# Another instruction order in the opening of a two-layer attention backbone, with five operands read from PSUM by ScalarE

## The chip, the core and the metric

The kernel runs on one core of a Trainium2 chip. The metric is the device time of one execution in microseconds (us); lower is better. Engines: TensorE (PE; its weight loads are PEld), VectorE (DVE), ScalarE (ACT), GpSimd (POOL) and SyncE (SP), which issues most of the DMA transfers. Each engine takes its instructions strictly in the order of its own queue and waits at the first whose semaphore has not come.

## The reference

Two layers over 1024 latent tokens (`x`) and 256 context tokens (`ctx`), model width 1024. Layer 0 is windowed attention with sink logits, layer 1 is latent attention. Cut to what the change touches:

```python
for i in range(DEPTH):
    shift_x, scale_x, gate_x = adaln(c, ada_w[i], ada_b[i])          # silu(c) @ ada_w + ada_b
    shift_c, scale_c, gate_c = adaln(c_ctx, ada_w[i], ada_b[i])
    hx = rms_norm(x, norm_g[i]) * (1.0 + scale_x[:, None]) + shift_x[:, None]
    hc = rms_norm(ctx, norm_g[i]) * (1.0 + scale_c) + shift_c
    yx, yc = window_gqa(hx, hc, a_w_in[j], ...)    # begins with q, k, v, g = split(h @ w_in)
    x = x + gate_x[:, None] * yx
    ...
```

All arithmetic is in float32. The products are made of a high part (rounded to the matmul's short format, `fp32r`) and a low part (the rest): high by high, high by low and low by high.

## The kernel before

The **opening** makes the normalized, conditioned and transposed input `h` of layer 0 for all tokens, and beside it the value projection `v`, the first 256 columns of the input projection. Tokens are worked in five blocks `p` of 256 (block 0 is the context), the 1024 features in four quarters `b`, so there are 20 **groups** `(p, b)`. The list `groups` (L932) gives their order: (0,0) (1,0) (2,0) (0,1) (1,1) (2,1) (3,0) (3,1) (4,0) (4,1), then the quarters 2 and 3 of all blocks.

For one block: `x_load` (L854) brings two tiles of 128 tokens, `square` (L860, ScalarE) and `norm` (L865, a small VectorE operation and a power on GpSimd) make the inverse root mean square, `scale` (L870, one half on VectorE or ScalarE each) applies it.

For one group there are four steps:

- `turn` (L877): four TensorE transposes into one PSUM bank, 5 or 7.
- `h_part` (L884): VectorE reads the bank twice, once for each 128 features (L890), times the scale plus the shift of the conditioning, into a buffer `h` in SBUF. Then one copy of all 512 columns (L892, ScalarE or GpSimd) makes the high part.
- `h_low` (L895): `h` minus the high part is the low part (L897, VectorE or GpSimd).
- `v_part` (L899): twelve matmuls, eight with the high part (L906) and four with the low part (L911).

Scale and shift of a quarter `q` come from a **conditioning step**: `ada_load` (L829) brings four pieces of `ada_w`, `ada_mm` (L835) multiplies each piece (four matmuls, L839), `ada_copy` (L843) moves the sums to SBUF on ScalarE, `ada_cols` (L846) spreads them as columns with two matmuls (L849) and three small VectorE operations (L328, L331). A group of quarter `q` can't pass `h_part` before `ada_cols(q)`. `w0_cut` (L927) splits two rows of the weights of `v` into high and low parts.

The opening stands between L947 and L1056 in a manual schedule: each engine gets its instructions in the order in which the code is written there, the two loops over the groups included; `make(i)` (L936) stands for the turn, the parts and the lows of the group `i`. A recording planner that orders instructions by costs (`Plan`, L68) is only switched on later (L1062). Tile's semaphores are set by the framework: it makes an engine wait for an earlier user of the same PSUM bank too.

After the opening come the other projections of layer 0 (matmuls L285 to L287), the attention, and layer 1.

## Time and profile before

| | |
|---|---|
| median of 3 runs | 1489.08 us (1487.2 to 1856.97) |
| profiled execution | 1487.75 us |
| its span, first to last instruction | 1485.6 us |
| TensorE, VectorE, ScalarE, GpSimd busy | 98%, 71%, 50%, 54% |
| products of groups in the opening (L906, L911) | 18.9 to 70.4 us |

How to read the rows: a timeline row has the start, the length, the engine, the line, the operation, what it writes and reads, and the count; in brackets stands the idle time of the engine before it and what ended that. A row of a group of instructions has its count, then its busy time and the mean of one in ns. A matmul's row lasts until its modelled end, so rows of TensorE that follow each other overlap a little, and the distance of two starts tells more than the lengths. A float32 matmul is recorded twice: a conditioning step's four matmuls of each of its four pieces are 32 records.

### The profile page before, as it was taken

How to read it: one execution, taken by the hardware profiler on the slowest of the kernel's cores; microseconds unless marked ns; L12 is line 12 of the kernel's file. 1: busy time of each engine (PE TensorE's matmuls, PEld its weight loads, DVE VectorE, ACT ScalarE, POOL GpSimd, SP SyncE). 2: the span in 40 equal slices, each digit the busy share in tenths (PEclk: the TensorE clock that was granted, in tenths of full speed). 3: DMA queues.
4: the chain of work that ended last, by engine and by line, in shares of the span. 5: the costliest groups of instructions: out<-in, count | busy, mean ns of one | idle time of the engine just before them, and what ended most of it. 6: DMA issues, size and time to landing. Idle time of an engine off the chain costs nothing.

```text
span 1485.6 us, 25066 instructions
## 1 busy us (share of the span) xinstructions
PE 1462.1 (98%) x9036; PEld 1186.8 (80%) x9036; DVE 1060.5 (71%) x2025; ACT 737.5 (50%) x1401; POOL 808.6 (54%) x735
## 2 busy tenths in 40 slices
PE   6999999999999999999999999999999999999998
PEld 4888888888888888889888888767777767866687
DVE  3787789648778888877988777666576466556764
ACT  4421222359888878877554432443454344444321
POOL 2563366356454444456300240798788788789371
PEclk9999999999999999999999999999999999999999
DMA  9545644573343333337344566011112212120442
GB/s 334 173 166 175 212 146 174 186 245 110 122 140 121 104 100 100 97 98 257 101 118 120 169 236 201 23 44 49 50 61 69 61 47 62 54 68 28 154 148 86
DMA packets 146964, 186.01 MB, mean 125 GB/s; under 512 B 12812, under 2 KB 100492, under 8 KB 146840
## 3 DMA queue, kind: packets, MB, share of 16 engines
q1 hardware_dynamic: 141864, 177.75, 37.9%
q10 hardware_dynamic: 4976, 6.66, 1.3%
q8 instruction: 71, 1.16, 0.3%
q14 instruction: 53, 0.43, 0.1%
HBM read 134.02 MB, written 46.15 MB: 121 GB/s over the span
## 4 chain that ended last, share of the span: by engine, by line
PE 90%; DVE 4%; DMA 2%; issue 1%; ACT 1%; POOL 0%; POOLq 0%; DVEq 0%; ACTq 0%
PE PB L285 14%; PE PB L286 14%; PE PB L287 14%; PE PB L1791 13%; PE PB L1814 9%; PE PB L737 5%; PE PB L1757 5%; PE PB L727 5%; PE PB L697 3%; PE PB L698 3%; DMA arena_f<-ada_w 1%; PE PB L1825 1%; PE PB L906 1%; DVE arena_r L281 1%; PE PB L756 1%
## 5 line engine op out<-in xcount | busy, mean ns | idle before, releaser
L285 PE MATMUL PB<-arena_r 128*128 128x512 f32 (+2 forms) x1200 | 439.4, 366 | 1.1 <-DVE arena_f L1239 1.1
L286 PE MATMUL PB<-arena_r 128*128 128x512 f32 (+2 forms) x1200 | 433.7, 361 | 0.0
L287 PE MATMUL PB<-arena_r 128*128 128x512 f32 (+2 forms) x1200 | 433.3, 361 | 0.0
L1807 POOL TENSOR_TENSOR arena_f<-arena_f 128x1024 f32<-128x1024 f32 x120 | 285.9, 2383 | 8.2
L285 PEld LDWEIGHTS PB<-arena_r 128*128 128x128 f32 x1200 | 226.3, 189 | 45.7 <-issue 9.0
L287 PEld LDWEIGHTS PB<-arena_r 128*128 128x128 f32 x1200 | 226.3, 189 | 33.5
L286 PEld LDWEIGHTS PB<-arena_r 128*128 128x128 f32 x1200 | 226.4, 189 | 32.1 <-POOL arena_r L281 0.6
L1791 PE MATMUL PB<-arena_r 64*128 64x512 f32 (+1 forms) x1600 | 229.3, 395 | 0.0
L1801 ACT ACTIVATE arena_f<-PB 128x1024 f32<-128x1024 f32 x160 | 164.5, 1028 | 111.7 <-PE PB L1791 84.9
L1763 DVE TENSOR_REDUCE krF<-PB 128x1 f32<-128x512 f32 (+1 forms) x264 | 166.9, 677 | 65.6 <-PE PB L1757 65.6
L1791 PEld LDWEIGHTS PB<-arena_r 64*128 64x128 f32 (+1 forms) x1600 | 178.2, 185 | 15.7 <-issue 5.2
L704 DVE CUSTOM_DVE_ANT_0 arena_f<-PB,arena_f,small 128x256 f32<-128x256 f32 (+1 forms) x288 | 148.1, 524 | 51.4 <-PE PB L698 32.8
L280 ACT CAST arena_r<-PB 128x512 fp32r<-128x512 f32 (+2 forms) x207 | 115.3, 563 | 113.2 <-PE PB L287 73.3
L281 DVE TENSOR_TENSOR arena_r<-PB,arena_r 128x512 fp32r<-128x512 f32 (+2 forms) x207 | 134.2, 660 | 35.1 <-ACT arena_r L280 34.4
L1814 PE MATMUL PB<-arena_f 128*64 128x512 f32 x640 | 146.0, 595 | 0.0
L281 POOL TENSOR_TENSOR arena_r<-arena_f,arena_r 128x512 fp32r<-128x512 f32 (+1 forms) x64 | 87.7, 1386 | 105.2 <-ACT arena_r L280 91.0
L280 ACT CAST arena_r<-arena_f 128x512 fp32r<-128x512 f32 (+1 forms) x142 | 82.3, 610 | 90.2 <-PE PB L287 27.8
L710 ACT ACTIVATE arena_f<-arena_f,small 128x640 f32<-128x640 f32 (+2 forms) x160 | 119.1, 745 | 15.8 <-DVE small L704 13.7
L507 DVE SCALAR_TENSOR_TENSOR arena_f<-arena_f,small 128x512 f32<-128x512 f32 x98 | 114.9, 1217 | 10.5 <-DMA arena_f<-ada_w 10.3
L737 PE MATMUL PB<-arena_r 128*128 128x512 f32 x336 | 118.7, 429 | 0.0
L1757 PE MATMUL PB<-arena_r 64*128 64x512 f32 (+1 forms) x768 | 113.9, 355 | 0.1
L727 PE MATMUL PB<-ident,arena_f 128*128 128x128 f32 x672 | 108.7, 272 | 0.1
(216 smaller groups left out, 2083.0 us busy)
## 6 DMA issues: line engine op xcount, KB each, us to landing
arena_f<-ada_w SPq DMA_DIRECT2D x96, 256.0 KB, 4.1
arena_r<-q_d SPq DMA_DIRECT2D x160, 128.0 KB, 2.8
arena_f<-a_w_in SPq DMA_DIRECT2D x40, 256.0 KB, 4.1
arena_f<-b_w_in SPq DMA_DIRECT2D x36, 256.0 KB, 3.3
arena_f<-x SPq DMA_DIRECT2D x16, 512.0 KB, 6.4
q_d<-arena_f SPq DMA_DIRECT2D x16, 512.0 KB, 3.0
arena_r<-qn_d SPq DMA_DIRECT2D x16, 512.0 KB, 5.1
g_d<-arena_f ACTq DMA_DIRECT2D x20, 256.0 KB, 4.1
```

Source lines behind the costliest of these rows:

```text
L280: nc.scalar.copy(hi, src)
L281: (lo_eng or nc.vector).tensor_sub(lo, src, hi.bitcast(F32))
L285: nc.tensor.matmul(o, ah, bh, start=first, stop=False)
L286: nc.tensor.matmul(o, al, bh, start=False, stop=False)
L287: nc.tensor.matmul(o, ah, bl, start=False, stop=last)
L727: nc.tensor.transpose(pt[:, h, :], self.Ps[h][:, ci * 128 : ci * 128 + 128], ident)
L737: nc.tensor.matmul(self.pv, V[:, self.chunks[ci], self.g, :], PT[:, s], start=ci == 0 and s == 0, stop=ci == self.m - 1 and s == 1,)
L1757: nc.tensor.matmul(bank[:, o : o + n], self.q[r, s, bs], k[r, 0, n0 : n0 + n], start=s == 0, stop=s == 2)
L1763: nc.vector.reduce_max(self.mxp[:, e, b : b + 1, i], bank[:, 0:n], AX.X)
L1791: nc.tensor.matmul(PB[:, b + e, :], k[r, s, cs], q[r, sq], start=i == 0, stop=i == 4)
L1807: eng.tensor_add(acc, acc, E)
L1814: nc.tensor.matmul(PB[r, 7, :], Vq[:, c, h, :], E[:, e], start=c == 0, stop=c == NT - 1)
```

## The change

- `h_part` gets two more forms. With `hi=None` ScalarE makes the high part itself, out of the PSUM bank (an `Identity` activation with scale and bias, one for each 128 features), beside VectorE's reading of the same bank into `h`. With `parts=2` the copy is made in two halves. Five groups take the first form: (1,0), (2,0), (0,1), (2,1) and (3,0). Group (0,0) takes the second, on GpSimd.
- `turn` and `v_part` run their inner loops in the other order: transposes token tile by token tile, high products feature block by feature block.
- `square` and `norm` can be done for one half of a block; blocks 1 and 2 use that.
- The order in the opening is rewritten up to group 8. Turn (1,1) stands ahead of the columns of conditioning step 1; the third conditioning step (`q = 2`) stands in one block behind the product of group (3,1), and turns (4,0) and (4,1) follow it, which stood behind the products of (3,0) and (3,1); the lows of (1,0), (1,1), (2,1) and (3,1) are made by VectorE, `w0_cut(1)` wholly by GpSimd.

SyncE's queue is the same in both. The lines of the helpers move: in the changed kernel L892 is ScalarE's reading of the bank, L894 and L897 are the copies, L902 the low part, L911 the high products and L916 the low products.

```diff
-    def norm(p):
+    def norm(p, j=0, n=2):
         _, sq, st = xn[p]
-        nc.vector.tensor_scalar(st[:, 0:2], sq[:, 0:2], 1.0 / D, EPS, ALU.mult, ALU.add)
-        nc.gpsimd.tensor_tensor(st[:, 2:4], st[:, 0:2], mhalf.to_broadcast([128, 2]), ALU.pow)
+        nc.vector.tensor_scalar(st[:, j : j + n], sq[:, j : j + n], 1.0 / D, EPS, ALU.mult, ALU.add)
+        nc.gpsimd.tensor_tensor(st[:, 2 + j : 2 + j + n], st[:, j : j + n], mhalf.to_broadcast([128, n]), ALU.pow)
...
-    def h_part(p, b, hi=nc.scalar.copy):
+    def h_part(p, b, hi=nc.scalar.copy, parts=1):
...
             nc.vector.tensor_scalar(h[:, kk], ps[:, kk], sa, sb, ALU.mult, ALU.add)
+            if hi is None:
+                nc.scalar.activation(hT[p][:, 0, k], ps[:, kk], AF.Identity, bias=sb, scale=sa)
+            elif parts == 2:
+                hi(hT[p][:, 0, k], h[:, kk])
         ks = slice(2 * b, 2 * b + 2)
-        hi(hT[p][:, 0, ks, :], h)
+        if hi and parts == 1:
+            hi(hT[p][:, 0, ks, :], h)
...
-        for j in range(2):
-            js = slice(j * 128, j * 128 + 128)
-            o = PB[:, p, j * 256 : j * 256 + 256]
-            for k in (2 * b, 2 * b + 1):
+        for k in (2 * b, 2 * b + 1):
+            for j in range(2):
+                js = slice(j * 128, j * 128 + 128)
+                o = PB[:, p, j * 256 : j * 256 + 256]
...
     v_part(0, 0)
     turn(1, 0, 7)
     square(2)
-    norm(2)
-    h_part(1, 0)
+    norm(2, 0, 1)
+    h_part(1, 0, None)
+    norm(2, 1, 1)
+    h_low(1, 0, nc.vector)
     scale(2, 0, nc.vector)
     scale(2, 1, nc.scalar)
-    w0_cut(1)
-    for kk in range(2):
-        ada_mm(1, kk)
-    h_low(1, 0, nc.vector)
+    w0_cut(1, nc.gpsimd.tensor_copy)
+    ada_mm(1, 0)
     v_part(1, 0)
+    ada_mm(1, 1)
     turn(2, 0, 5)
-    ada_mm(1, 2)
-    h_part(2, 0)
+    h_part(2, 0, None)
     h_low(2, 0, nc.vector)
+    ada_mm(1, 2)
     ada_mm(1, 3)
     ada_copy()
     turn(0, 1, 7)
+    turn(1, 1, 5)
     ada_cols(1)
...
     v_part(2, 0)
-    turn(1, 1, 5)
-    h_part(0, 1, nc.gpsimd.tensor_copy)
+    h_part(0, 1, None)
     square(3)
     h_low(0, 1, nc.vector)
-    norm(3)
-    h_part(1, 1)
-    h_low(1, 1)
+    h_part(1, 1, nc.gpsimd.tensor_copy)
...
+        v_part(p, q)
         if i == 3:
+            turn(2, 1, 7)
+            h_part(2, 1, None)
+            norm(3)
+            h_low(1, 1, nc.vector)
+            h_low(2, 1, nc.vector)
             scale(3, 0, nc.vector)
             scale(3, 1, nc.scalar)
-        v_part(p, q)
-        if i < 8:
-            make(i + 2)
-        if i == 3:
+        if i == 4:
+            turn(3, 0, 5)
+            h_part(3, 0, None)
+            h_low(3, 0)
             square(4)
-            norm(4)
         if i == 5:
+            turn(3, 1, 7)
+            h_part(3, 1, nc.gpsimd.tensor_copy)
+            norm(4)
+            h_low(3, 1, nc.vector)
             scale(4, 0, nc.vector)
             scale(4, 1, nc.scalar)
-            ada_mm(2, 0)
-            ada_mm(2, 1)
             w0_cut(2)
-        if i == 6:
-            ada_mm(2, 2)
-            ada_mm(2, 3)
-            ada_copy()
-            w0_cut(3)
         if i == 7:
+            for kk in range(4):
+                ada_mm(2, kk)
+            ada_copy()
+            make(8)
+            make(9)
             ada_cols(2)
+            w0_cut(3)
```

Where instructions come to stand, at three places. The rows have the line, the operation, what is written and read, the shape, and in brackets the engines or DMA queues whose semaphores the row waits for (the number behind a name is the framework's).

**VectorE and ScalarE at groups (1,0) and (2,0).** L890 reads the bank, L897 (later L902) makes the low part, L867 and L875 belong to the normalization of block 2; on ScalarE L892 makes the high part, L873 scales, L929 cuts weights, L844 copies the conditioning sums. Before, VectorE and then ScalarE:

```order
L867 TENSOR_SCALAR small<-small 128x2 [waits Activation_49]
L890 TENSOR_SCALAR arena_f<-PB,small 128x256 [waits PE_49]
L890 TENSOR_SCALAR arena_f<-PB,small 128x256
L875 TENSOR_SCALAR arena_f<-arena_f,small 128x1024 [waits DMAHW2_49,Pool_49]
L897 TENSOR_TENSOR arena_r<-arena_f,arena_r 128x512 [waits Activation_49]
```

```order
L892 CAST arena_r<-arena_f 128x512 [waits DVE_49]
L873 ACTIVATE arena_f<-arena_f,small 128x1024 [waits Activation_49,Pool_49]
L929 CAST arena_r<-arena_f 128x512 [waits DMAHW4_49]
L892 CAST arena_r<-arena_f 128x512 [waits DVE_49]
L844 COPY arena_f<-PB 98x256 [waits PE_49]
```

Now:

```order
L867 TENSOR_SCALAR small<-small 128x1 [waits Activation_49]
L890 TENSOR_SCALAR arena_f<-PB,small 128x256 [waits PE_49]
L890 TENSOR_SCALAR arena_f<-PB,small 128x256 [waits Activation_49]
L867 TENSOR_SCALAR small<-small 128x1
L902 TENSOR_TENSOR arena_r<-arena_f,arena_r 128x512 [waits Activation_49]
L875 TENSOR_SCALAR arena_f<-arena_f,small 128x1024 [waits DMAHW2_49,Pool_49]
```

```order
L892 ACTIVATE arena_r<-PB,small 128x256 [waits DVE_49] x2
L873 ACTIVATE arena_f<-arena_f,small 128x1024 [waits Activation_49,Pool_49]
L892 ACTIVATE arena_r<-PB,small 128x256 [waits DVE_49] x2
L844 COPY arena_f<-PB 98x256 [waits PE_49]
L892 ACTIVATE arena_r<-PB,small 128x256 [waits DVE_49,PE_49]
```

Each of ScalarE's two readings now waits for VectorE's reading of the same half, and VectorE's second reading waits for ScalarE's first.

**VectorE at groups (1,1) and (2,1).** Before, from the low part of (0,1) on:

```order
L897 TENSOR_TENSOR arena_r<-arena_f,arena_r 128x512 [waits Pool_49]
L867 TENSOR_SCALAR small<-small 128x2 [waits Activation_49]
L890 TENSOR_SCALAR arena_f<-PB,small 128x256 [waits PE_49]
L890 TENSOR_SCALAR arena_f<-PB,small 128x256
L875 TENSOR_SCALAR arena_f<-arena_f,small 128x1024 [waits DMAHW5_49,Pool_49]
```

Now, from the low part of (0,1) on:

```order
L902 TENSOR_TENSOR arena_r<-arena_f,arena_r 128x512 [waits Activation_49]
L890 TENSOR_SCALAR arena_f<-PB,small 128x256 x2
L890 TENSOR_SCALAR arena_f<-PB,small 128x256 [waits DVE_49,PE_49]
L890 TENSOR_SCALAR arena_f<-PB,small 128x256 [waits Activation_49]
L867 TENSOR_SCALAR small<-small 128x2
L902 TENSOR_TENSOR arena_r<-arena_f,arena_r 128x512 [waits Pool_49]
L902 TENSOR_TENSOR arena_r<-arena_f,arena_r 128x512 [waits Activation_49]
L875 TENSOR_SCALAR arena_f<-arena_f,small 128x1024 [waits DMAHW5_49,Pool_49]
```

The two lows of (1,1) and (2,1), which GpSimd made before, and the normalization of block 3 (L867, L875) stand behind both readings of (2,1).

**TensorE from the product of (3,0) to the product of (4,0)** (the first row pair and the last row). Before:

```order
L906 MATMUL PB<-arena_r 128x256 x8
L911 MATMUL PB<-arena_r 128x256 x4
L882 MATMUL PB<-ident,arena_f 128x128 x4
L839 MATMUL PB<-arena_f,small 2x256 x8
L906 MATMUL PB<-arena_r 128x256 x8
L911 MATMUL PB<-arena_r 128x256 x4
L882 MATMUL PB<-ident,arena_f 128x128 x4
L849 MATMUL PB<-small,arena_f 128x34 x2
L882 MATMUL PB<-ident,arena_f 128x128 x4
L906 MATMUL PB<-arena_r 128x256 x8
```

Now:

```order
L911 MATMUL PB<-arena_r 128x256 x8
L916 MATMUL PB<-arena_r 128x256 x4
L911 MATMUL PB<-arena_r 128x256 x8
L916 MATMUL PB<-arena_r 128x256 x4
L839 MATMUL PB<-arena_f,small 2x256 x16
L882 MATMUL PB<-ident,arena_f 128x128 x8
L849 MATMUL PB<-small,arena_f 128x34 x2
L882 MATMUL PB<-ident,arena_f 128x128 x4
L911 MATMUL PB<-arena_r 128x256 x8
```

The sixteen conditioning matmuls, of which eight stood ahead of the product of (3,0) and eight between the two products, and the turns of block 4 now follow the product of (3,1).

30 lines of the change are left out of this document (16 added, 14 removed).

## The prediction

> **What bounds the kernel now.** I read the page first, then the busy time of two stretches, then TensorE's timeline through the opening, then the chain of waits there.
>
> ```profile
> span 1485.6 us, 25066 instructions
> PE   6999999999999999999999999999999999999998
> ```
>
> TensorE is busy in every slice behind the first. A change confined to the first 50 us can only win or lose what TensorE waits for there, and what it wins or loses moves all that follows.
>
> ```profile
> 18.90:45.50 26.60, 24.75 (x207) 19.46 (x208) 15.90 (x33) 16.09 (x27) 14.12 (x14) 0.94 0.96 319
> 45.50:70.40 24.90, 24.90 (x226) 23.18 (x225) 18.65 (x41) 11.49 (x24) 12.66 (x10) 1.00 0.57 184
> ```
>
> The first number behind the stretch is its length, the next TensorE's busy time. From 45.5 on TensorE never waits; before that it does. Busy time hides part of it, since a matmul's row lasts to a modelled end. The starts say more:
>
> ```profile
> 18.94 2.08 PE L906 MATMUL PB<-arena_r 128*128 128x256 f32 x8 [2.28 <-POOL arena_r L892]
> 21.67 0.71 PE L882 MATMUL PB<-ident,arena_f 128*128 128x128 f32 x4
> 25.92 0.60 PE L882 MATMUL PB<-ident,arena_f 128*128 128x128 f32 x4
> 26.45 1.04 PE L839 MATMUL PB<-arena_f,small 128*2 128x256 f32 x16
> 27.42 0.66 PE L882 MATMUL PB<-ident,arena_f 128*128 128x128 f32 x4
> 30.51 0.60 PE L882 MATMUL PB<-ident,arena_f 128*128 128x128 f32 x4
> 33.00 0.60 PE L882 MATMUL PB<-ident,arena_f 128*128 128x128 f32 x4
> 35.76 0.60 PE L882 MATMUL PB<-ident,arena_f 128*128 128x128 f32 x4
> 37.62 0.60 PE L882 MATMUL PB<-ident,arena_f 128*128 128x128 f32 x4
> 44.39 0.60 PE L882 MATMUL PB<-ident,arena_f 128*128 128x128 f32 x4
> 44.83 0.53 PE L849 MATMUL PB<-small,arena_f 98*128 98x34 f32 x4
> 45.19 0.63 PE L882 MATMUL PB<-ident,arena_f 128*128 128x128 f32 x4
> 45.58 1.19 PE L906 MATMUL PB<-arena_r 128*128 128x256 f32 x8
> 47.45 1.19 PE L906 MATMUL PB<-arena_r 128*128 128x256 f32 x8
> ```
>
> Where nothing is late, a product and a turn take 47.45 - 45.58 = 1.87 us, of it the turn 0.44 (44.39 to 44.83), so eight high matmuls take 0.96 and four low ones 0.48. Two pieces of a conditioning step take 0.97 (26.45 to 27.42), the columns 0.36. From 18.94 to 45.58 stand the first product (2.73, to 21.67), seven more with a turn each (13.1), three more turns (1.3), eight pieces (3.9) and two columns (0.7): 21.7 of 26.6 us. So TensorE's waits there are worth **4.9 us**, the most that a better order could take away, beside an earlier start. Who holds it up:
>
> ```profile
> 26.55 1.01 DVE arena_f L890 x2
> 27.59 0.62 ACT arena_r L892
> 28.20 0.28 ACT arena_f L844
> 30.80 0.62 POOL arena_r L892
> 35.24 1.15 ACT arena_r L863 x2
> 38.71 0.63 ACT arena_r L892
> 39.40 1.30 POOL arena_r L897
> ```
>
> These are rows of the chain that ended last: VectorE's pair of readings, the one copy behind it (ScalarE or GpSimd), the copy of the conditioning sums, squares that hold ScalarE, a low part on GpSimd.
>
> **The change part by part.** The prices:
>
> ```profile
> L890 DVE TENSOR_SCALAR arena_f<-PB,small 128x256 f32<-128x256 f32 x20 | 9.9, 538 | 5.4 <-PE PB L882 3.3 <-POOL arena_r L897 2.0
> L1464 ACT ACTIVATE arena_f<-PB,small 128x256 f32<-128x256 f32 x20 | 10.2, 561 | 3.6 <-DVE arena_f L1465 3.5
> L917 ACT CAST arena_r<-PB 128x256 fp32r<-128x256 f32 x10 | 3.0, 384 | 0.8 <-PE PB L911 0.8
> L892 ACT CAST arena_r<-arena_f 128x512 fp32r<-128x512 f32 x7 | 4.3, 618 | 9.3 <-DVE arena_f L890 9.3
> L897 DVE TENSOR_TENSOR arena_r<-arena_f,arena_r 128x512 fp32r<-128x512 f32 x4 | 2.8, 692 | 1.4 <-POOL arena_r L892 0.7 <-ACT arena_r L892 0.7
> L763 POOL CAST arena_r<-arena_f 128x256 fp32r<-128x256 f32 x39 | 15.5, 398 | 2.5
> L873 ACT ACTIVATE arena_f<-arena_f,small 128x1024 f32<-128x1024 f32 x3 | 3.4, 1148 | 0.0
> 37.84 0.69 POOL L868 TENSOR_TENSOR small<-small 128x2 f32<-128x2 f32 x1 [1.15 <-DVE small L867]
> ```
>
> ScalarE's new instruction, an `Identity` out of a bank with scale and bias, stands in layer 1 already (L1464): 0.56. And there it shares its bank with VectorE (L1465), as the change has it now:
>
> ```profile
> 689.19 0.54 DVE L1465 TENSOR_SCALAR arena_f<-PB,small 128x256 f32<-128x256 f32 x1
> 689.76 0.57 ACT L1464 ACTIVATE arena_f<-PB,small 128x256 f32<-128x256 f32 x1
> 690.59 0.57 ACT L1464 ACTIVATE arena_f<-PB,small 128x256 f32<-128x256 f32 x1
> 691.19 0.54 DVE L1465 TENSOR_SCALAR arena_f<-PB,small 128x256 f32<-128x256 f32 x1 [0.69 <-ACT arena_f L1464]
> ```
>
> The readings don't overlap: the second starts 0.03 behind the end of the first, and VectorE sat 0.69 idle for ScalarE. The order shown above has the same waits, so the five **direct groups** read in single file: VectorE 0.54, ScalarE 0.56, VectorE 0.54, ScalarE 0.56, with a hand-over of 0.04 ahead of each. The first half of the high part is ready 1.18 behind the turn, the second 2.36, the low part 3.1. Before, the whole high part was ready at 0.04 + 1.01 + 0.04 + 0.62 = 1.71 and a low part on VectorE at 2.45. So a direct group hands over the first half 0.53 earlier and the rest 0.65 later, and the bank, and VectorE's queue behind the second reading, are held as long.
>
> Now the walk, on the clock of the trace; "ready" is a turn's last start plus its 0.15 of drain (a row's 0.60 against 0.44).
>
> First product: the first half is read 0.47 before the pair's end and its copy is 0.21 shorter, so it starts 0.7 before 18.94, at 18.3, and turn (1,0) ends at 21.7 instead of 22.4. The normalization of block 1 in halves stays in front of that turn.
>
> (1,0): ready 21.7, halves at 22.9 and 24.05, low 24.8, product to 25.3, the piece that was put behind it to 25.8; turn (2,0) then stands where it stood before, at 25.92. **The 0.7 is spent.**
>
> (2,0): turn to 26.25, ready 26.4; two pieces and turn (0,1) fill TensorE to 27.65. Turn (1,1) needs bank 5, which the four readings hold until 28.75: 1.1 us of idleness that the old order, with the columns there, filled in part. Turn, columns and product (2,0) last to 31.0; before, the same work ended at 30.95. Even.
>
> (0,1): its columns end at 29.55 and 0.15, three small operations take 0.5, the halves are ready at 31.35 and 32.55, the low at 33.3, the product ends at 33.8, before at 33.0. **0.8 behind.**
>
> (1,1): copied by GpSimd in 0.61 to 34.85, high products to 35.8. Its low stands on VectorE behind both readings of (2,1), whose turn ends at 34.25: 34.4 + 0.04 + 0.54 + 0.60 + 0.58 = 36.15, then 0.69, low products 36.9 to 37.35, before 35.7. **1.65 behind.**
>
> (2,1): ahead of its product stands turn (3,0), which needs block 3 scaled; that normalization stands behind the same readings: small operation, power 0.69, scaling 1.15 on ScalarE, 38.15. Turn and product end at 40.05, before 37.6. **2.45 behind.**
>
> (3,0), (3,1): turn (3,1) to 40.5; (3,0) was ready at 38.75, halves at 39.95 and 41.1, the low on GpSimd (1.30) at 42.45, product to 42.95. Only then GpSimd copies (3,1), 43.1; VectorE's low of it waits for the squares of block 4 (two of 1.15 behind 41.1), ready 44.25, product to 44.75, before 44.39.
>
> By then the old order had done four pieces and turn (4,0) more. These take 1.95 and 0.44, with turn (4,1) 0.44 and the columns 0.36: 47.95. Turn (0,2) waits for VectorE's pair on bank 5 (ready 47.3, free 48.3) and ends at 48.8; the high part of (4,0) comes at 48.95, its low from GpSimd at 50.3, so the product of (4,0) starts at 49.0 (before 45.58) and that of (4,1) at 51.3, before 47.45. **The end of the walk: 3.85 behind**, with as many instructions for TensorE as before. Behind that point both orders are alike, and the old one had no wait there.
>
> The other moves cost nothing here. `w0_cut(1)` wholly on GpSimd ends near 26, 5 us before product (0,1) needs those weights; late by more than that, it would hold TensorE. SyncE's queue is the same, but the pieces of the last quarter of `ada_w` wait for the buffers of the third step:
>
> ```profile
> arena_f<-ada_w SPq DMA_DIRECT2D x96, 256.0 KB, 4.1
> ```
>
> They are let go from 45.2 on, about 0.4 apart; the first four land by 51, the product that stands ahead of their use ends near 52.7. If this cover of 1.7 were gone, the rest would add to the loss.
>
> **Sum:** the profiled execution took 1487.75 (the median of the runs, 1489.08, lies 1.3 above it); 1487.75 + 3.85 = 1491.6. ScalarE's reading is bounded by 0.38 (L917, out of a bank without pointers) and 0.62 (the copy): nine of them lie on the walk, so -1.6 to +0.5. I take L1464, the same operation. With those ends: 1490.0 to 1492.1; and the lowest run and the median lie 1.9 apart.
>
> **The rivals.** *The single file is hidden* (not slower). If VectorE's second reading went on beside ScalarE's first, five groups would have the rest 0.7 earlier and most of the walk's loss would go: 3.85 - 5 x 0.7 = 0.35, so 1488.1. It decides if the second reading starts less than 0.1 behind the first. Against it stand the rows at 690.59 and 691.19 and the waits in the order; for it only that VectorE's own pairs overlap. 0.10. The Trainium skill, "PSUM — Partial Sum Buffer", section "PSUM bank collisions raise a hardware error", says that two engines must not touch one bank and quadrant at once, reads included; by it this rival falls away, and the trace agrees (0.69 of idleness at 691.19).
>
> *The loss is given back later* (no change, 1488): if a later stage waited for transfers that don't move with the opening. For it, nothing; against it TensorE's full slices. 0.08.
>
> *A second stretch at half clock* (worse still).
>
> ```profile
> 15.10:18.50 3.40, 1.03 (x12) 0.52 (x4) 1.39 (x5) 2.49 (x5) 1.95 (x3) 1.00 1.03 408
> 18.50:21.90 3.40, 2.96 (x14) 2.96 (x15) 2.38 (x5) 2.47 (x6) 1.69 (x3) 0.50 1.08 352
> ```
>
> The granted clock (third from the end) fell to 0.50 for 3.4 us after a stretch in which TensorE worked 1.03 of 3.4. In the walk it works 1.4 of the 3.4 us from 34.25 on, less than anywhere in the old order after 22. If that is little enough, the next 3.4 us go at half speed, and some 1.7 us of matmuls take twice as long: 1493.3. 0.12. The Trainium skill, "TensorE: Matmul & The Clock Gate", section "Part 1: The HAM clock gate", has the same length, 3413 ns, and says that the window runs free, so that its phase differs between executions; the trace shows the length, one execution can't show the phase.
>
> **How the numbers follow.** The forecast, slower by some 4 us, gets 0.66, the three rivals 0.10, 0.08 and 0.12, anything else 0.04. The predicted time is 1491.6. The range reaches down to the middle of the two cases near 1488 and up past the half clock by part of that scatter: 1488.0 to 1494.4. 2% are 30 us, about what a measurement here can tell from no change; no case comes near it, so faster 0.01, same 0.98, slower 0.01.
>
> **What would show it.** Right: L892 on ScalarE near 0.56, VectorE's second L890 starting 0.6 behind the end of the first in the direct groups; turn (1,1) waiting about 1 us for ScalarE; the product of (4,1) starting near 51; no wait of TensorE from there to 74; the span longer by 3 to 5 us. Wrong: a pair of readings less than 1.2 us long, the product of (4,1) before 48, or a span that doesn't follow the opening.

## The result, and the profile after

The changed kernel takes 1492.42 us, the median of 7 runs (1492.02 to 1494.41), against 1487.79 for the kernel before, run beside it: 1.0031 times as long, with a 95% interval of 1.002 to 1.0042. One of the seven runs of the kernel before took 1856.97, in a slow state, and is left out here and in the ratio; with it the median is 1488.35. At a bound of 2% that is no change; by the interval, which leaves 1 out, it is a small, clear loss of some 4.6 us. The time is 0.8 above the predicted 1491.6.

The page of the changed kernel answers to the two lines shown of before: the span is 4.4 us longer, and again TensorE is busy in every slice behind the first.

```profile
span 1490.0 us, 25078 instructions
...
PE   6999999999999999999999999999999999999998
```

The two stretches of the opening, on each engine: length, then TensorE's busy time, at the end granted clock and DMA. In the first TensorE is busy for 22.36 of 26.6 us, where it was 24.75; from 51.3 on, 22.96 of 23 us, it waits no more.

```profile
18.90:45.50 26.60, 22.36 (x156) 16.76 (x156) 15.25 (x33) 14.50 (x25) 9.84 (x11) 0.90 0.76 258
51.30:74.30 23.00, 22.96 (x209) 21.38 (x209) 16.97 (x36) 10.80 (x24) 12.87 (x10) 1.00 0.68 218
```

TensorE's timeline (start, length, line; L911 are high products, L916 low ones, L882 turns; in brackets the idle time ahead and who ended it):

```profile
17.79 2.08 PE L911 MATMUL PB<-arena_r 128*128 128x256 f32 x8 [2.13 <-POOL arena_r L894]
...
23.08 1.65 PE L911 MATMUL PB<-arena_r 128*128 128x256 f32 x8
...
29.01 0.66 PE L882 MATMUL PB<-ident,arena_f 128*128 128x128 f32 x4 [0.85 <-ACT arena_r L892]
...
29.87 1.19 PE L911 MATMUL PB<-arena_r 128*128 128x256 f32 x8
...
34.36 0.60 PE L882 MATMUL PB<-ident,arena_f 128*128 128x128 f32 x4
...
37.44 0.74 PE L916 MATMUL PB<-arena_r 128*128 128x256 f32 x4 [0.87 <-DVE arena_r L902]
38.79 0.83 PE L882 MATMUL PB<-ident,arena_f 128*128 128x128 f32 x4 [0.62 <-DVE arena_f L875]
39.38 1.19 PE L911 MATMUL PB<-arena_r 128*128 128x256 f32 x8
...
49.97 1.22 PE L911 MATMUL PB<-arena_r 128*128 128x256 f32 x8
...
52.27 1.20 PE L911 MATMUL PB<-arena_r 128*128 128x256 f32 x8
```

Before, the products of (1,0), (2,0), (2,1) and (3,1) started as follows:

```profile
24.38 1.22 PE L906 MATMUL PB<-arena_r 128*128 128x256 f32 x8
...
29.00 1.20 PE L906 MATMUL PB<-arena_r 128*128 128x256 f32 x8
...
36.11 1.19 PE L906 MATMUL PB<-arena_r 128*128 128x256 f32 x8
...
42.85 1.22 PE L906 MATMUL PB<-arena_r 128*128 128x256 f32 x8
```

Product by product against the starts of before: (0,0) at 17.79, 1.15 earlier; (1,0) at 23.08, 1.3 earlier than its 24.38; (2,0) at 29.87, 0.9 later than its 29.00; (2,1) at 39.38, 3.3 later than its 36.11; (4,1) at 52.27, 4.8 later than 47.45. From there to the end of the opening the distance stays at 4.8. The loss is made between 23 and 52 us, mainly by two kinds of wait that the brackets name: for ScalarE's readings of a bank (L892, 1.7 us in all), and for VectorE's low part and scaling behind them (L902 and L875, 1.5 us). Another 1.2 us of waits are for GpSimd's copies and low parts.

The single file is plain to see in group (2,0), on VectorE's and ScalarE's timelines:

```profile
26.63 0.55 DVE L890 TENSOR_SCALAR arena_f<-PB,small 128x256 f32<-128x256 f32 x1 [0.95 <-PE PB L882]
27.21 0.57 ACT L892 ACTIVATE arena_r<-PB,small 128x256 fp32r<-128x256 f32 x1 [2.00 <-DVE arena_f L890]
27.81 0.54 DVE L890 TENSOR_SCALAR arena_f<-PB,small 128x256 f32<-128x256 f32 x1 [0.64 <-ACT arena_r L892]
28.39 0.56 ACT L892 ACTIVATE arena_r<-PB,small 128x256 fp32r<-128x256 f32 x1 [0.61 <-DVE arena_f L890]
```

Each reading starts 0.03 or 0.04 behind the end of the other engine's, and either engine is idle for 0.6 in between. Four readings hold bank 5 from 26.63 to 28.95, and turn (1,1), which needs the bank, starts at 29.01.

### The profile page after: what moved, and what is told of

Read it like the earlier page. It is cut to its first block, busy times and chain, and to the rows that moved or that the text cites. A ratio compares the mean times of both kernels' runs of the same rounds, so it can differ in the third digit from the quotient of the medians.

```text
span 1490.0 us, 25078 instructions
## 1 busy us (share of the span) xinstructions
PE 1465.3 (98%) x9036; PEld 1186.6 (80%) x9036; DVE 1062.2 (71%) x2030; ACT 739.3 (50%) x1404; POOL 807.6 (54%) x737
## 4 chain that ended last, share of the span: by engine, by line
PE 91%; DVE 5%; issue 1%; ACT 1%; DMA 1%; POOL 1%; POOLq 0%; DVEq 0%; SPq 0%; ACTq 0%
PE PB L285 14%; PE PB L286 14%; PE PB L287 14%; PE PB L1805 13%; PE PB L1828 9%; PE PB L737 5%; PE PB L1771 5%; PE PB L727 5%; PE PB L697 3%; PE PB L698 3%; PE PB L911 1%; PE PB L1839 1%; DVE arena_r L281 1%; DMA arena_f<-ada_w 1%; PE PB L839 1%
## 5 line engine op out<-in xcount | busy, mean ns | idle before, releaser
L1805 PE MATMUL PB<-arena_r 64*128 64x512 f32 (+1 forms) x1600 | 226.6, 395 | 0.0
L1805 PEld LDWEIGHTS PB<-arena_r 64*128 64x128 f32 (+1 forms) x1600 | 174.9, 185 | 16.6 <-issue 5.2
L1771 PE MATMUL PB<-arena_r 64*128 64x512 f32 (+1 forms) x768 | 111.2, 355 | 0.1
```

The lines of the kernel that those rows point to most:

```text
L1771: nc.tensor.matmul(bank[:, o : o + n], self.q[r, s, bs], k[r, 0, n0 : n0 + n], start=s == 0, stop=s == 2)
L1805: nc.tensor.matmul(PB[:, b + e, :], k[r, s, cs], q[r, sq], start=i == 0, stop=i == 4)
```

## The experiments

Two theories stood against each other, A (single file) and B (the order), beside C (the clock). One table first, so that each experiment can be read against it. Starts of three products in the profiled execution, the stretches of the opening in which the granted clock was 0.50, and the timed runs beside the kernel before (difference of the medians, ratio with its interval); all times in us.

| kernel | (0,0) | (2,0) | (4,1) | half clock | median | ratio |
|---|---|---|---|---|---|---|
| before | 18.94 | 29.00 | 47.45 | 18.5-21.9 | | |
| before, again (e5) | 18.30 | 28.63 | 47.10 | 16.8-23.7 | | |
| the change | 17.79 | 29.87 | 52.27 | 17.1-24.0 | +4.6 | 1.0031 [1.002, 1.0042] |
| the change, again (e6) | 18.17 | 30.24 | 53.23 | 19.5-22.9, 40.0-43.4 | | |
| e1, change with one copy | 18.20 | 29.71 | 50.28 | 18.8-22.2 | +3.1 | 1.0023 [1.0013, 1.0033] |
| e2, before with direct form | 18.20 | 29.36 | 51.90 | 18.8-22.2 | +4.4 | 1.0035 [1.0023, 1.0048] |
| e3, change with TensorE kept busy | 17.45 | 29.27 | 52.25 | 39.1-42.5 | +5.1 | 1.0038 [1.0025, 1.0052] |
| e4, before with the block | 17.97 | 28.32 | 48.24 | 18.5-21.9 | +1.3 | 1.0012 [1.0004, 1.0021] |
| e7, one copy, no block | 17.80 | 29.06 | 49.23 | 17.4-20.8 | +2.7 | 1.0018 [1.001, 1.0027] |
| e8, old order, halves | 17.15 | 29.52 | 47.44 | 22.5-25.9 | -0.6 | 0.9994 [0.9985, 1.0003] |
| e9, e8 with TensorE kept busy | 18.00 | 29.12 | 47.04 | none | -0.9 | 0.999 [0.9981, 0.9999] |
| e10, change, ScalarE first | 17.32 | 29.05 | 53.09 | 16.8-20.2, 37.3-44.1 | +4.7 | 1.0033 [1.002, 1.0045] |
| e11, before with the first step | 17.36 | 29.67 | 48.78 | 18.5-25.4 | +0.9 | 1.0004 [0.9995, 1.0013] |
| e12, e9 with one copy moved | 17.82 | 28.49 | 46.40 | none | -1.6 | 0.9988 [0.9979, 0.9997] |

**e1: the change without the single file**, in groups (1,0), (2,0), (0,1), (2,1) and (3,0) alike.

```diff
 # the change
-    h_part(1, 0, None)
+    h_part(1, 0)
```

> The changed kernel, order and all, but the five direct groups (1,0), (2,0), (0,1), (2,1), (3,0) read their bank by VectorE's pair alone, with one ScalarE copy of 128x512 behind it, as before the change. Theory A (single file: the bank read in turns by two engines is most of the loss): the low part comes 0.65 earlier in five groups and the bank is free 1.2 us earlier, so the walk of the prediction, done over with 1.71 and 2.45 in place of 2.36 and 3.1, puts the product of (4,1) 1.5 us behind the kernel before: at 49.0, against 52.27 with the change; span about 1487.1. Theory B (the order is the loss: the third conditioning step in one block, low parts moved to VectorE): the product stays near 52 and the span near 1489.5. Theory C (the longer stretch at half clock is the loss): the same as B, as long as the half clock still lasts 6.8 us.

TensorE's timeline, the product of (4,1), and TensorE's waits from 17 to 52 us (in total, times, longest):

```profile
50.28 1.19 PE L911 MATMUL PB<-arena_r 128*128 128x256 f32 x8
```

```profile
PE PB L911 <- ACT arena_r L897: 1.9, 2, 1.0
...
PE PB L882 <- DVE arena_f L875: 1.0, 2, 0.6
PE PB L916 <- DVE arena_r L902: 0.4, 1, 0.4
```

50.28 lies between A's 49.0 and the 52 of B and C. Of the 4.8 us that the opening lost, the single file takes 2.0 (52.27 - 50.28); 2.8 stay without it. So A alone falls as the whole cause, and so does B. C is not tested here, as the half clock lasted 3.4 us and not 6.8. The timed runs (+3.1 against +4.6) point the same way, but their intervals overlap, so the size of 2.0 rests on single traces. One thing differs from before in this kernel too: the high part of (0,1) is copied by ScalarE, where GpSimd did it.

**e2: the kernel before with the direct form in the same five groups.**

```diff
 # the kernel before
             nc.vector.tensor_scalar(h[:, kk], ps[:, kk], sa, sb, ALU.mult, ALU.add)
+            if hi is None:
+                nc.scalar.activation(hT[p][:, 0, k], ps[:, kk], AF.Identity, bias=sb, scale=sa)
...
-    h_part(1, 0)
+    h_part(1, 0, None)
```

> The kernel before with nothing changed but the form of the same five groups: ScalarE reads the bank beside VectorE. Theory A: single file alone makes this slower, in this order even by more than in the changed one, since the pieces that the old order put ahead of the products give no cover; the walk puts the product of (4,1) 5.3 us later: at 52.7 instead of 47.45, span about 1491, and the second reading of VectorE starts 0.6 behind the end of its first. Theory B: less than 1 us, at 48, span 1486 to 1486.5.

VectorE's timeline in group (2,0):

```profile
26.25 0.54 DVE L890 TENSOR_SCALAR arena_f<-PB,small 128x256 f32<-128x256 f32 x1 [1.27 <-PE PB L882]
27.43 0.54 DVE L890 TENSOR_SCALAR arena_f<-PB,small 128x256 f32<-128x256 f32 x1 [0.64 <-ACT arena_r L892]
```

The second reading starts 0.64 behind the end of the first (26.25 + 0.54 = 26.79), and the product of (4,1) starts at 51.90, 4.5 later than in the first profile of before and 4.8 later than in the second; A said 5.3, B less than 1. Alone, in the order that it was not made for, the single file costs as much as the whole change. Not all of it is the taking of turns. TensorE's longest wait here, 2.06 us at the product of (1,1), is for ScalarE's copy. That copy and VectorE's readings ahead of it come late because ScalarE's squares of block 3 stand behind its readings of (0,1), a group that GpSimd copied before; the squares begin at 32.38, before at 28.38. So the direct form also costs by its work on ScalarE, and no run separates the two. The costs of form and order don't add (2.0 in the new order, 4.5 here); that the other delays of the new order cover a part is argued, not shown.

**e3: the change with TensorE kept busy ahead of the first product.**

```diff
 # the change
     ada_cols(0)
+    for _ in range(14):
+        nc.tensor.transpose(PB[:, 7, 0:128], ident, ident)
```

> The changed kernel with 14 additional transposes of the identity (128x128, nobody reads them) into the bank of the next turn, behind the first columns, where TensorE waits from 15.7 to 17.8 for the first high part. At 0.11 each they take 1.6 us and end before 17.8. Theory C: the clock fell to 0.50 for 6.8 us since TensorE worked only 1.3 of 3.4 us ahead of it; with 2.8 of 3.4 it stays at 1.00. The walk with and without the half clock differs by 0.76 us behind product (1,0), so the product of (4,1) starts at 51.5 instead of 52.27 and the span is 1489.2. If all of the loss were the clock: 47.5 and 1485.6. If the fill does not touch the clock: 0.50 stays, 52.3, span 1490.

Busy time by stretch (length, TensorE, weights, VectorE, ScalarE, GpSimd; then the granted clock):

```profile
15.17:18.58 3.41, 2.88 (x24) 2.51 (x23) 2.62 (x9) 2.62 (x5) 2.41 (x4) 1.00 1.02 401
18.58:22.00 3.42, 2.46 (x14) 1.12 (x16) 2.08 (x5) 2.38 (x5) 1.54 (x2) 1.00 1.10 351
...
35.65:39.07 3.42, 1.94 (x13) 1.35 (x12) 2.49 (x6) 1.71 (x2) 1.08 (x1) 1.00 0.59 187
39.07:42.48 3.41, 3.41 (x18) 3.41 (x17) 1.22 (x3) 2.19 (x5) 1.01 (x1) 0.50 0.00 0
```

The fill kept the clock at 1.00 from 15 to 39 us, as C has it. But the next stretch with little work, 1.94 of 3.42 us while TensorE waits for the low part of (1,1) and the scaling of block 3, brought the half clock back at 39.07. The product of (2,1) was 0.6 earlier than in the change (38.78 against 39.38), that of (4,1) starts at 52.25: the gain was gone. So the clock isn't the cause of most of the loss: at the product of (2,1), with the clock at 1.00 from 15 us on, this execution is 2.7 behind before (38.78 against 36.11), which had 3.4 us at half clock. The half clock follows the waits.

**e4: the kernel before with the third conditioning step in one block.**

```diff
 # the kernel before
-            ada_mm(2, 0)
-            ada_mm(2, 1)
...
-        if i == 6:
-            ada_mm(2, 2)
-            ada_mm(2, 3)
-            ada_copy()
-            w0_cut(3)
         if i == 7:
+            for kk in range(4):
+                ada_mm(2, kk)
+            ada_copy()
             ada_cols(2)
+            w0_cut(3)
```

> The kernel before with one move: the eight pieces of the third conditioning step stand in one block behind product (3,1), as in the change, with the third cut of the weights behind the columns. Theory B: the pieces no longer fill TensorE's waits between (2,1) and (3,1), the walk puts the product of (4,1) 1.6 us later, at 49.0 instead of 47.45, span 1487.2. If single file is all of the loss (A alone): no difference, 47.5 and 1485.6.

```profile
48.24 1.20 PE L906 MATMUL PB<-arena_r 128*128 128x256 f32 x8
```

This execution began early: it ran 0.67 ahead of before from product (1,0) to product (3,0), and was 0.79 behind at (4,1). The block therefore cost 1.46 of the 1.6 that B gave it, and the timed runs show it (1.0012, [1.0004, 1.0021]). B holds for this part: a part of the loss has nothing to do with a bank.

**e5 and e6: both kernels once more, unchanged.**

> The kernel before, unchanged, in one more profiled execution. What is asked: how far the start of the first product (18.94 in the first profile, 17.97 in that of the kernel with the block moved, which differs nowhere ahead of it) and the phase of the half clock differ between executions. If both are set by the kernel, 18.9, with the clock at 0.50 from 18.5 to 21.9, and the product of (4,1) at 47.45. If by the execution, the first product anywhere from 17.9 to 19.2, and the product of (4,1) up to 0.7 off.

> The changed kernel, unchanged, in one more profiled execution. If the 6.8 us at half clock belong to the kernel, they come again, and the product of (4,1) starts at 52.3. If they belong to the phase of a window that runs free, 3.4 us or none behind the first product, and the product of (4,1) up to 0.8 earlier, at 51.5.

The clock belongs to the execution. Before, it was at 0.50 for 3.4 us in one profile and 6.8 in the other, and the product of (4,1) moved by 0.35 only. In the second profile of the change, busy time by stretch and TensorE's product of (4,1):

```profile
36.59:40.00 3.41, 1.94 (x13) 1.34 (x13) 2.51 (x5) 1.71 (x2) 1.08 (x1) 1.00 0.42 138
40.00:43.41 3.41, 3.41 (x18) 3.41 (x18) 1.17 (x3) 2.16 (x4) 0.98 (x1) 0.50 0.00 0
```

```profile
53.23 0.95 PE L911 MATMUL PB<-arena_r 128*128 128x256 f32 x6
```

The prediction's third rival, a second stretch at half clock near the place where it was looked for, is what this execution shows; the first had 2.15 us of work in the stretch from 34.20 to 37.62 and kept its clock. Its price is small: the two executions are 0.36 apart at (2,1) and 0.96 at (4,1), so 0.6. The rule cited in the prediction from the Trainium skill ("TensorE: Matmul & The Clock Gate", section "Part 1: The HAM clock gate"), that the window runs free and its phase differs between executions, agrees with this: the half clock begins at 17.1 in one execution of the change and at 19.5 in the other.

**e7: the change without single file and without the block.** The pieces stand behind the products of (2,1) and (3,0), as before the change.

```diff
 # e1
             scale(4, 1, nc.scalar)
+            ada_mm(2, 0)
+            ada_mm(2, 1)
             w0_cut(2)
+        if i == 6:
+            ada_mm(2, 2)
+            ada_mm(2, 3)
+            ada_copy()
         if i == 7:
-            for kk in range(4):
-                ada_mm(2, kk)
-            ada_copy()
```

> The changed kernel without single file (one ScalarE copy in the five groups) and with the third conditioning step spread again over two places, behind products (3,0) and (0,2) where the order of products has them, as before the change. With one copy but the block, the product of (4,1) started at 50.28, 2.8 behind the kernel before. Theory A+B: single file and the block are all that costs; the block was worth 1.5 from product (1,0) to product (4,1) in the old order, so the product of (4,1) starts at 48.8 or before (the walk: 48.3), 0.8 to 1.4 behind. Theory D: the low parts and the early turn of (1,1) that wait on VectorE cost as much as the block; then it stays at 50.

TensorE's timeline, (1,1)'s low products, turn (3,0) and the product of (4,1):

```profile
35.47 0.74 PE L916 MATMUL PB<-arena_r 128*128 128x256 f32 x4 [0.43 <-DVE arena_r L902]
36.84 0.81 PE L882 MATMUL PB<-ident,arena_f 128*128 128x128 f32 x4 [0.63 <-DVE arena_f L875]
...
49.23 1.20 PE L911 MATMUL PB<-arena_r 128*128 128x256 f32 x8
```

49.23 lies short of what A+B expected (48.3 to 48.8) and is better than D (50). 1.8 of the loss remain with neither single file nor block, and the timed runs show a loss too (1.0018, [1.001, 1.0027]).

The trace puts the remainder at two places. The first are the two rows shown, where VectorE makes the low parts of (1,1) and (2,1) and the scaling of block 3 one behind another: the product of (1,1) starts level with before (33.82 against 33.81), that of (2,1) 1.3 later. The second is behind the product of (3,1), where the turns (4,0) and (4,1) now stand. The products of (3,1) and (4,0) in e7:

```profile
43.04 1.22 PE L911 MATMUL PB<-arena_r 128*128 128x256 f32 x8
...
46.92 1.22 PE L911 MATMUL PB<-arena_r 128*128 128x256 f32 x8
```

(3,1) is only 0.2 behind (42.85 before), though the turn (4,0), 0.44, is then still to be done; (4,0) is 1.3 behind (45.58 before), and (4,1) 1.8. In between turn (0,2) waits for VectorE's readings and the low products of (4,0) for GpSimd, since block 4 was turned late. So more than half of the remainder arises there. That these moves cost it is argued from the rows; no kernel undid them alone.

From before to e7 to e1 to the change the product of (4,1) goes 47.45, 49.23, 50.28, 52.27. The step from e7 to e1 isn't the block alone: up to the product of (2,1) both have the same code, and e7 is 0.64 ahead there already (37.41 against 38.05). That leaves 0.4 for the block in this order (1.46 in the old one, e4), as between the timed medians (+2.7 and +3.1). So the loss of 4.8 is made of **1.8 to 2.4 for the other moves, 0.4 for the block, 2.0 for the single file**, each with the 0.6 or so by which single executions differ.

**e10: the direct form with ScalarE first.** ScalarE reads both halves, then VectorE both.

```diff
 # the change, in h_part
+        if hi is None:
+            for e in (nc.scalar, nc.vector):
+                for kk in range(2):
...
+                    if e is nc.scalar:
+                        e.activation(hT[p][:, 0, k], ps[:, kk], AF.Identity, bias=sb, scale=sa)
+                    else:
+                        e.tensor_scalar(h[:, kk], ps[:, kk], sa, sb, ALU.mult, ALU.add)
```

> The change with another order of readers in the five direct groups: ScalarE reads both halves (0.56 each), then VectorE both. The first half of the high part is ready at 0.6 behind the turn and the second at 1.2, in place of 1.18 and 2.36 with turns taken (and 1.71 with one copy); the low part at 2.9 and the bank free at 2.2, nearly as with turns taken. Theory A1 (the late second high half is what single file costs): the product of (4,1) comes 2 us or more earlier than the 52.3 to 53.2 of the change, near 50. Theory A2 (it is the bank held for 2.2 us and the late low part, while VectorE waits for ScalarE): only the 0.2 of the low part per group, 0.8 by the walk: 51.4 and span 1489.2.

ScalarE's pair of readings in group (2,0), VectorE's behind it, and TensorE's longest wait from 17 to 52 us (L910 is the low part here):

```profile
26.09 1.02 ACT L893 ACTIVATE arena_r<-PB,small 128x256 fp32r<-128x256 f32 x2 [0.53 <-PE PB L882]
```

```profile
27.14 1.00 DVE L895 TENSOR_SCALAR arena_f<-PB,small 128x256 f32<-128x256 f32 x2 [2.80 <-ACT arena_r L893]
28.18 0.69 DVE L910 TENSOR_TENSOR arena_r<-arena_f,arena_r 128x512 fp32r<-128x512 f32 x1
```

```profile
PE PB L924 <- DVE arena_r L910: 2.6, 3, 1.2
```

Here the whole high part is ready at 27.1, 1.0 behind the start of the readings, sooner than in any other form. Up to the product of (1,1) that is a lead of 1.1 over the change (34.27 against 35.35); at turn (3,0) the lead is down to 0.15 (38.64 against 38.79), and in the end it brings nothing: 53.09, with 6.8 us at half clock in the middle, and the ratio of the change itself. A1 falls. TensorE has the high part and then waits for the low, which needs VectorE's own readings (2.6 us in three waits). So the late high part isn't what single file costs; the rows point to the low part, VectorE's queue and the bank, which all wait for the last of four readings.

**e11: the first step of the change alone** (block (0,0) in two copies, loops by half, block 1 normalized in two steps).

```diff
 # the kernel before
-    h_part(0, 0, nc.gpsimd.tensor_copy)
-    square(1)
-    norm(1)
+    h_part(0, 0, nc.gpsimd.tensor_copy, 2)
+    square(1, [0])
+    norm(1, 0, 1)
     h_low(0, 0, nc.vector)
+    square(1, [1])
+    norm(1, 1, 1)
```

> The kernel before with the change's first step alone: block (0,0) copied by GpSimd in two halves, the high matmuls and the transposes by half, squares and norm of block 1 in two steps. The prediction has it that the first product starts 0.7 earlier and that this is spent by product (1,0) or (2,0). By the walk the product of (0,1) and all after it come 0.5 later, (4,1) at 48.0, span 1486.1. If the start is kept: 46.7 and 1484.9. The start itself differs by 0.6 to 1.0 between executions, so the distance from the first product to the product of (4,1) is what counts: 28.5 before and 28.8 in its second profile.

First product at 17.36, product of (4,1) at 48.78, with 6.8 us at half clock behind the first product. From the one to the other are 31.4 us, where before had 28.5 and 28.8, so the earlier start isn't kept: by product (1,0) this execution is 0.4 behind before. Part of the reason are two pieces of conditioning step 1 ahead of that product. From 20 to 26 us the weight loads of TensorE wait for their transfers:

```profile
PEld PB L839 <- DMA arena_f<-ada_w: 2.5, 4, 0.7
```

Before, this was 1.3, and the last wait ended at the same time (23.84; here 23.85). An earlier first product alone can't move the product behind pieces that have not come. Whether e11 is a loss stays open, since the interval of its ratio holds 1.

**e8, e9 and e12: the early half without a second reader.** e8 keeps the old order and VectorE alone on the bank, and copies each of the first eight high parts in two halves (the diff shows the first of them).

```diff
 # e11
-    h_part(1, 0)
-    w0_cut(1)
-    for kk in range(2):
-        ada_mm(1, kk)
+    h_part(1, 0, nc.scalar.copy, 2)
...
+    w0_cut(1, nc.gpsimd.tensor_copy)
     h_low(1, 0, nc.vector)
+    ada_mm(1, 0)
     v_part(1, 0)
+    ada_mm(1, 1)
```

> A version for the better: the old order and the bank read by VectorE alone, but each high part of the first eight groups copied in two halves (the first behind VectorE's first reading), the product's high matmuls by half, the first cut of block 1 in halves as in the change, and the second step's first two pieces around product (1,0). Theory A: what the change wanted, an early first half, is to be had without a second reader of the bank: first half ready at 1.0 and second at 1.5 behind the turn in place of 1.71, and the bank free after 1.05; the walk puts the product of (4,1) 1.3 before the kernel before, at 46.15, span 1484.3, ratio 0.999. If earlier high parts do not matter, since low parts or late squares hold TensorE anyway: 47.5, span 1485.6. If two copies of 128x256 cost ScalarE more than they bring: 48 or later.

Busy time by stretch:

```profile
19.06:22.47 3.41, 1.72 (x12) 0.59 (x12) 2.37 (x6) 2.49 (x6) 1.78 (x3) 1.00 1.09 357
22.47:25.89 3.42, 3.42 (x18) 2.68 (x12) 2.46 (x2) 1.27 (x2) 1.84 (x2) 0.50 1.11 359
```

No faster at (4,1): 47.44. The half clock fell on product (1,0), and 1.4 us of lead became 0.5 of lag at (2,0). (VectorE's low part of (1,0) took 1.76 here too, which e9 explains.) So e9 fills TensorE's idle time:

```diff
 # e8
     ada_cols(0)
+    for _ in range(14):
+        nc.tensor.transpose(PB[:, 7, 0:128], ident, ident)
...
     turn(1, 0, 7)
+    for _ in range(5):
+        nc.tensor.transpose(PB[:, 5, 0:128], ident, ident)
```

> The version with halves on VectorE's readings (e8), with 14 transposes of the identity that nobody reads behind the first columns and 5 more behind turn (1,0), where TensorE waits. In e8 the product of (1,0) began 1.40 before that of the kernel before and that of (2,0) 0.52 behind it, with the clock at 0.50 from 22.5 to 25.9 in between, after a stretch with 1.72 of 3.4 us busy. Theory C: the half clock took the gain. With TensorE kept busy the clock stays at 1.00 there, the product of (2,0) starts about 28.0 and that of (4,1) near 46.1, span 1484.2, ratio 0.998. If low parts and squares decide anyway: (2,0) earlier, (4,1) still 47.4. If the half clock only moves to a later stretch, as in e3: between the two.

The clock stayed at 1.00 through the opening, in the mean 0.999 to 1.000 of the span in all 11 runs. Yet the product of (4,1) starts at 47.04, where 46.1 was expected. VectorE, GpSimd and TensorE in e9:

```profile
23.16 1.77 DVE L902 TENSOR_TENSOR arena_r<-arena_f,arena_r 128x512 fp32r<-128x512 f32 x1
```

```profile
22.76 1.62 POOL L935 TENSOR_TENSOR arena_r<-arena_f,arena_r 128x512 fp32r<-128x512 f32 x1
```

```profile
24.98 0.74 PE L916 MATMUL PB<-arena_r 128*128 128x256 f32 x4 [1.08 <-DVE arena_r L902]
```

VectorE's low part of (1,0) took 1.77, against 0.69 for that of (2,0), with GpSimd's subtraction of the weights beside it, and TensorE waited 1.08 for it. By the timed runs e9 can't be told from e8; both medians are 1486.91. e12 moves GpSimd's work away from there:

```diff
 # e9
-    w0_cut(1, nc.gpsimd.tensor_copy)
+    w0_cut(1)
```

> The version with halves and a busy TensorE (e9) with one copy moved back: the high part of the second quarter of the weights (the first step of w0_cut(1)) on ScalarE behind its scaling of block 2, as before the change, in place of GpSimd. In e9 GpSimd's subtraction of that cut (22.76, 1.62) and VectorE's low part of (1,0) (23.16) ran at once, and the low part took 1.77 in place of 0.69; TensorE waited 1.1 for it. Theory E: GpSimd and VectorE hold each other up. The subtraction then starts only near 25, VectorE's low part takes 0.69, the wait of 1.1 goes and with it 1.1 of the start of product (4,1): 46.0, span 1484.7 and ratio 0.998 or a little over. If 1.77 had another cause: no change, (4,1) at 47.0, ratio 0.999. If the cut comes too late for product (0,1) (needs it near 30) or collides with VectorE's readings of (2,0): a new wait of about 1 there and nothing won.

VectorE, then GpSimd:

```profile
23.02 0.69 DVE L902 TENSOR_TENSOR arena_r<-arena_f,arena_r 128x512 fp32r<-128x512 f32 x1
```

```profile
24.50 1.27 POOL L935 TENSOR_TENSOR arena_r<-arena_f,arena_r 128x512 fp32r<-128x512 f32 x1 [2.19 <-ACT arena_r L934]
```

The low part is back at 0.69, the wait of 1.08 is gone, and turn (2,0) starts 1.1 earlier than in e9 (25.10 against 26.20), as theory E has it. The product of (4,1) starts at 46.40, 1.05 before the kernel before and 0.6 before e9: the rest goes in new waits for the pieces of conditioning step 1 (1.0 us of TensorE's weight loads, up to 26.90). With 0.9988 [0.9979, 0.9997] this version has the lowest ratio of all here and beats both kernels, if by little; from e9 the timed runs don't separate it. Part of the gain goes at the start of layer 1, near 684 us, where the trace falls from 1.3 to 0.6 ahead of before. TensorE's wait there, before and in e12:

```profile
PE PB L1457 <- DVE arena_f L1465: 0.5, 1, 0.5
```

```profile
PE PB L1468 <- DVE arena_f L1476: 1.2, 1, 1.2
```

## Why the prediction was right, and where its steps were off

**The bound** held: nothing but the opening moves, and what it loses goes through to the end.

**The single file** held as described: 0.56 for ScalarE's reading, 0.03 or 0.04 for the hand-over, the second reading 0.6 behind the first, turn (1,1) held by ScalarE for 0.85 by the bracket, or 29.01 - 27.94 = 1.07 counted from starts, as the predicted 1.1 is.

**The walk** found the waits in their places and was short in size. Its numbers against the first profile of the change: first product 18.3, measured 17.79; the piece behind product (1,0) 25.3, measured 25.39; turn (1,1) 28.75, measured 29.01; (1,1)'s low products 36.9, measured 37.44; turn (3,0) 38.15, measured 38.79; product of (4,0) 49.0, measured 49.97; product of (4,1) 51.3, measured 52.27. The sum of 3.85 was 4.8. It is no single term: the delay grows from 0.3 at turn (1,1) to 0.6 at turn (3,0) and 1.0 at (4,0). That the walk is so close up to 25.39 is partly luck: the first product came 0.5 earlier than the walk has it, and from there to turn (2,0) it took 8.1 in both executions of the change, where the walk has 7.6.

**"The other moves cost nothing here"** and the power of 0.69 overlooked that VectorE and GpSimd hold each other up. VectorE's two low parts, then GpSimd's power for block 3, and VectorE's scaling of that block, in the change:

```profile
36.70 1.34 DVE L902 TENSOR_TENSOR arena_r<-arena_f,arena_r 128x512 fp32r<-128x512 f32 x2
36.87 1.07 POOL L868 TENSOR_TENSOR small<-small 128x2 f32<-128x2 f32 x1 [1.57 <-DVE small L867]
37.98 0.75 DVE L875 TENSOR_SCALAR arena_f<-arena_f,small 128x1024 f32<-128x1024 f32 x1
```

The power took 1.07 beside the low parts, 0.38 more than alone. ScalarE's half of block 3 waited 0.67 for it, and with it the second half of turn (3,0); VectorE's half stood behind the two low parts anyhow. So the price is small: the product of (2,1) starts 0.59 behind that turn's start, where 0.36 is usual, and this is one of the links that were too short. `w0_cut(1)` on GpSimd cost the change nothing that shows, as there turn (2,0) was not waiting. In e1 and e7 VectorE's scaling of block 2 took 1.77 beside it and turn (2,0) waited 0.41, and in e9 the same step cost 1.08.

**The 0.7 of the first product.** The profile of before started later (18.94) than any other execution with the same code ahead of the first product (18.30, 18.20 and 17.97). Its mean over these four is 18.35, and over the ten executions with the first copy in halves 17.7, so 0.65 is about right, and so is that it is spent: (2,0), said to be even, is 0.9 late in the change, and in e11 the lead is gone at (1,0).

**The rivals.** Hidden single file: out, by the timeline and by e2. Given back later: in the change 0.37 of 4.83 came back by the end of the span; other executions lost up to 1.7 more in the middle (e1: 1.1 near 330 us, 0.6 at the start of layer 1), so this is scatter and gives nothing back. The second stretch at half clock was given 0.12 and a price of 1.7. It came in the second profile, one of two, at a price of 0.6. How often it comes the timed runs don't settle: two of the seven runs of the change have a mean clock of 0.994 and are the slowest (1493.89 and 1494.41), but both traces of the change have a higher one (0.997 and 0.996), and the kernel before has such runs too (0.995, 1490.10 and 1490.43, beside e12). Forecast and rival are thus no alternatives: the same kernel can go either way from one execution to the next.

**The timed median** is 4.6 over before while the product of (4,1) is 4.8 or 5.8 late against the first profile of before, and 5.2 or 6.1 against the second, which is 0.35 earlier. The sum of 3.85 is thus short by either count. What comes and goes in the middle of the span (0.4 back in the first profile of the change) makes up some of the difference between the two.

## What to carry to other kernels

Two engines that read one bank in turns finish it later than one engine that reads it all (2.32 against 1.01 us here), and what counts is the last reading, which frees the bank and starts the low part, not the first. Before giving an engine a second piece of a bank, copy the first half from what the first engine has already written: that has an early half as well and leaves the bank to one reader. (By itself it brought nothing clear here: e8, 0.9994 [0.9985, 1.0003].) When work moves between engines, look for what runs on VectorE and GpSimd at the same time, and in a stretch where TensorE waits, the clock can fall too.

## What the runs showed of the hardware

**VectorE and GpSimd.** A subtraction of 128x512 on VectorE takes 0.69 and took 1.77 beside one on GpSimd (1.62 in place of 1.27); a power of two columns on GpSimd took 1.07 in place of 0.69. In e9 VectorE's subtraction ended at 24.93, 0.55 behind the end of GpSimd's at 24.38. The Trainium skill ("SBUF — State Buffer", section "SBUF: two separate sides") says that the two share a pair of ports by an exclusive lock, and that whichever comes second, if it needs them, is blocked until the first has finished. The rows agree: 24.93 less 0.69 is 24.24, about the end of GpSimd's. And 24.38 less 1.27 is 23.11, about the end of VectorE's scaling ahead of it (22.50 + 0.74).

**The clock.** From 11 us on, and counted in steps of 3.41 us from a start of half clock, stretches at full clock in which TensorE was busy for 1.72 us or less were followed by half clock (0.65 to 1.72 in eleven executions), those with 2.15 or more were not. Between them it went both ways: 1.84 once and 1.94 twice to half clock, 1.81 (e8) and 1.91 (e2) not. At half clock already, the next stretch stayed there behind 1.94 to 2.77 us of busy time and came back behind 2.92 or more. What the chip counts, a busy time with a modelled end can't say.

**The start of layer 1.** TensorE waits there for VectorE, 0.2 to 1.2 us from one execution to the next; two executions that differ by less can't be told apart by their spans.
